# Two token streams of a float32 decoder trunk: products emitted in turn instead of unit by unit, small tiles moved to a pool of their own

## The chip, the cores and the metric

The kernel runs on one core of one Trainium2 chip. The metric is the device time of one execution in microseconds; the median of three runs of the kernel before is 1221.22 us (1220.48 to 1221.98). TensorE (PE in the profile, with its weight loads as PEld) multiplies, VectorE (DVE), ScalarE (ACT) and GpSimd (POOL) do the rest, and SyncE (SP) issues the loads of the weights.

## The reference

Four decoder layers over 256 tokens of width 1024. Layer i has a token mixer of kind i mod 3, then a SwiGLU FFN with 2816 hidden columns; each is wrapped in two RMSNorms:

```python
for i in range(DEPTH):
    kind = i % N_MIXERS
    ...
    hn = rms_norm(x, norm_gains[i, 0])
    if kind == 0:
        m = diff_attention(hn, ...)
    elif kind == 1:
        m = stick_breaking_attention(hn, ...)
    else:
        m = sliding_window_sink_attention(hn, ...)
    x = x + rms_norm(m, norm_gains[i, 1])
    f = swiglu(rms_norm(x, norm_gains[i, 2]), ffn_w_gate[i], ffn_w_up[i], ffn_w_down[i])
    x = x + rms_norm(f, norm_gains[i, 3])
```

Every mixer is an input projection, an attention over 256 keys, and an output projection. All of it is float32, and the weights are read once, some 204 MB.

## The kernel before, in words

**Two streams.** The 256 tokens are two blocks of 128. Stream 0 works on the first block and stream 1 on the second, each through all four layers (`stream`, L900 to L924). Both use the same weights, and the keys and values of the first block are used by the second.

**Products.** A float32 operand is split into two float32r parts, hi and lo, and a product is three matmuls (hi times hi, hi times lo, lo times hi). For the weights, ACT copies a loaded tile into `hi` and DVE writes the rest into `lo` (`split`, L252). For the tokens, `xh` and `xl` (`pre_norm`, L416), `oh` and `ol`, `hTh` and `hTl` (`split_rows`) play the same part. Tokens are the stationary operand, weights the moving one, with 512 columns as a rule.

**Units.** The weights come in units of 128 x 1024 float32, in one list in the order of use (L187 to L236). A unit is loaded by SP into one of 4 stage buffers, split into one of 11 ring buffers, and used by both streams. A unit is 6 matmuls of 512 columns for each stream: in `project` (L494) all 6 add to one PSUM bank (tag `mm`, one bank per stream; the first chunk of a projection uses a bank of the tag `acc`), in `rows_product` (L468) they add to two banks (tag `acc`, two banks per stream), turn by turn. A chunk of a projection is 4 units: 24 matmuls into one bank. An FFN is 11 such chunks, with the down projection of chunk c-1 (2 units) behind chunk c from c = 1 on; the down projections of the last three chunks come at the end.

**The order of the work.** The program is unrolled in Python. Each stream is a generator, and `Emitter.run` (L123) decides which one emits next. A generator yields `("w",)` when it needs its next unit, `("d", ns)` to be resumed no earlier than that many ns of emitted TensorE work later, and `("e", key)` to wait for an event. Between two yields it emits without a break, so that a unit's 6 matmuls come out together. The clock of the emitter, `em.t`, adds 1/2.4 ns per column, 213 ns for a matmul of 512. Attention runs in further generators (tasks) that are resumed as soon as their time or event has come.

Of the two streams, `run` takes the first that can go on, in this order:

```python
behind = any(self.pos[1] < w <= self.pos[0] for w in self.edges)
order = mains[::-1] if behind else mains
```

`pos[s]` is the number of units that stream s has taken. So stream 0 comes first, except while it has passed an edge that stream 1 has not. Edges stand after each layer's input projection (L228) and after each layer's FFN (L236). `can` (L112) lets stream 0 lead by up to LAG = 8 units and lets stream 1 take only units that stream 0 has taken. Around the norms a stream waits: `stream` yields `("d", 4000)` after `post_norm` (L914, L921) and `("d", 600)` after `pre_norm` (L906, L917). There are two norm stops in a layer, one after the mixer and one after the FFN; the last FFN has none behind it, which makes 7.

A scheduler below the emission may still move an instruction past others that it takes to be ready earlier; otherwise each engine runs in the order of emission.

**Where tiles lie.** Tiles are packed in the order of their pools and tags, each padded to a multiple of 32 bytes per partition. Tiles of one to eight floats therefore shift what follows by 32 bytes. In the program of before, the ring's `hi` and `lo`, `oh`, `ol`, `hTh`, `hTl`, and `xh`, `xl` of stream 1 start at multiples of 64 bytes; `xh` and `xl` of stream 0, the identity `ident` (the moving operand of the transposes), its bf16 copy `identb`, the masks and the residual `x` start 32 bytes past one.

**Names in the profile.** `mm_b100q` is the chunk of layer kind b, layer 1, stream 0, group 0, part q. Names that end in digits lose them, so that all FFN chunks of both streams are `mm_f`, all down projections `acc_f`. `th_f` are the FFN's transposes, `tp_n` and `tp_q` those of `pre_norm`, `t_f` and `h_f` the gated activations, `junk_e` the squares in `post_norm` after an FFN, `mg_e` the accumulators times the gain.

Of the kernel before, what the change touches and what calls it, by code (L numbers as in the profile page):

```python
# [9 lines left out]
F32 = mybir.dt.float32  # L10
# [8 lines left out]
P = 128  # L19
# [21 lines left out]
class Emitter:  # L41
    """Orders the emission of several generators by a running estimate of the tensor engine's time.

    A generator yields ("w",) for the next weight unit, ("d", ns) to be resumed no earlier than ns
    after the tensor engine's work emitted so far, or ("e", key) to wait for an event.
    """

    def __init__(self, load_dma, split, n_units, edges):
        self.t = 0.0
        self.load_dma, self.split, self.n, self.edges = load_dma, split, n_units, edges  # L50
        self.issued = self.loaded = 0
        self.pos = [0, 0]
        self.ring = {}
        self.events = set()
        self.limit = 0
        self.tasks = []
# [32 lines left out]
    def run_main(self, m):  # L89
        s = m["s"]  # L90
        value = None
        if m["want"] == "w":
            u = self.pos[s]
            value = self.ring[u]
            self.pos[s] += 1
            if s == 1:
                self.ring.pop(u)
            m["want"] = None
        try:
            what = m["gen"].send(value)  # L100
# [57 lines left out]
def trunk_kernel(ctx, tc, x, positions, norm_gains, a_w_in, a_w_out, a_lambda, a_subln, b_w_in, b_w_out,  # L158
# [5 lines left out]
    wk = ctx.enter_context(tc.tile_pool(name="wk", bufs=2))  # L164
    ps = ctx.enter_context(tc.tile_pool(name="ps", bufs=1, space=PSUM))
# [4 lines left out]
    class Start:  # L170
        """An engine whose instructions stay in the order of emission until the start is over."""
# [40 lines left out]
    def downs(c):  # L212
        """The chunks of the down projection that follow chunk c of the gate and up projections."""
# [55 lines left out]
    pos_i = cst.tile([P, 2], I32, name="pos_i")  # L269
# [10 lines left out]
    nsink = cst.tile([P, 16], F32, name="nsink")  # L280
# [4 lines left out]
    inv = cst.tile([P, 32], F32, name="inv")  # L285
    mhalf = cst.tile([P, 8], F32, name="mhalf")
    quarter = cst.tile([P, 1], F32, name="quarter")
    pool.memset(quarter, math.pi / 2)
    act.activation(wk.tile([P, 1], F32, tag="preload", name="preload", bufs=1), quarter, AF.Sin)
# [7 lines left out]
    # additive masks of a block of keys: causal, strictly causal, and the part of the window before the block  # L297
# [12 lines left out]
    gsub = cst.tile([P, 2], F32, name="gsub")  # L310
    lam_init = [0.8 - 0.6 * math.exp(-0.3 * i) for i in (0, 3)]
    nlam = cst.tile([P, 2], F32, name="nlam")
# [3 lines left out]
    def tables():  # L316
        """Generator: cos twice and sin with its sign, per position."""
        magic = 12582912.0
        posf = cst.tile([P, 2], F32, name="posf")
# [28 lines left out]
    def scalars():  # L348
        """-lambda, the negated sinks, and the gains of the inner norm."""
        lsum = wk.tile([P, 4], F32, tag="lsum", name="lsum", bufs=1)  # L350
# [28 lines left out]
    def mm3(o, ah, al, bh, bl, first, last):  # L379
        mm(o, ah, bh, first, False)  # L380
        mm(o, ah, bl, False, False)
        mm(o, al, bh, False, last)

# [4 lines left out]
    def rstd_of(name, s, ss, more=EPS, extra=None):  # L388
        """1/rms from the mean square, or from two parts of it."""
        u = wk.tile([P, 1], F32, tag=f"u{s}", name=f"u_{name}")  # L390
        r = wk.tile([P, 1], F32, tag=f"r{s}", name=f"r_{name}", bufs=3)
# [4 lines left out]
    def first_halves(s, tps, gs, th, tl, name):  # L396
        """The parts of the first layer's input, between the steps of the tables and the first weights."""
# [57 lines left out]
    def post_norm(s, acc, gain, name):  # L455
        ss = wk.tile([P, 2], F32, tag=f"ssp{s}", name=f"ssp_{name}")
# [23 lines left out]

    def out_proj(s, oT, name, last):
        """Generator: the product of the transposed rows in oT with the next 8 row units, into two banks."""
        acc = None
        for kt in range(KT):
# [6 lines left out]
            rows_product(acc, oh, ol, w, kt == 0, kt == KT - 1)  # L491
# [29 lines left out]
    def scaled_tables(s, r, name):  # L521
        """The tables of the keys, and those of the queries, which carry the scores' scale."""
# [24 lines left out]
    def score_products(s, sc, q, k, mask):  # L547
        """The scores of two pairs of heads: the heads of even and of odd number, in half of the array's rows and a bank each."""
# [13 lines left out]
    def split_rows(oT, sl, src, scale=None):  # L562
        """src, times scale, as two float32r parts."""
# [8 lines left out]
    def layer_a(s, i, xn):  # L572
# [20 lines left out]
        def scores(g):  # L593
# [5 lines left out]
            l = st[g] = wk.tile([P, 2, 4], F32, tag=f"l{s}", name=f"l_{name}{g}", bufs=2)  # L599
            el = st[g, "el"] = wk.tile([P, 4], F32, tag=f"el{s}", name=f"el_{name}{g}", bufs=2)  # L600
            ws = {}
            for step in range(3):
                if step < 2:
# [5 lines left out]
                    nm = wk.tile([P, 2, 2], F32, tag=f"nm{s}", name=f"nm_{name}{g}{h0}")  # L609
# [9 lines left out]
                    r = wk.tile([P, 2], F32, tag=f"rl{s}", name=f"rl_{name}{g}{h0}")  # L619
# [19 lines left out]
        def values(g):  # L639
# [8 lines left out]
            ss = wk.tile([P, 4], F32, tag=f"os{s}", name=f"os_{name}{g}")  # L648
# [124 lines left out]
    def layer_c(s, i, xn):  # L773
# [19 lines left out]
        def heads(chunk, g):  # L793
# [17 lines left out]
            nm = wk.tile([P, 2, 2], F32, tag=f"nm{s}", name=f"nm_{name}{g}")  # L811
            es = wk.tile([P, 2, 2], F32, tag=f"es{s}", name=f"es_{name}{g}")
            l = wk.tile([P, 2, 2], F32, tag=f"l{s}", name=f"l_{name}{g}")
# [43 lines left out]
    def ffn(s, i, xn):  # L857
        name = f"f{i}{s}"
        half = wk.tile([P, 1], F32, tag=f"half{s}", name=f"half_{name}", bufs=1)
        hsq = wk.tile([P, 1], F32, tag=f"hsq{s}", name=f"hsq_{name}", bufs=1)  # L860
# [5 lines left out]
        def down(c):  # L866
            nonlocal acc
            for j in range(2):
# [4 lines left out]
                rows_product(acc, hT[c][0][:, j2, :], hT[c][1][:, j2, :], w, c == 0 and j == 0, c == NCH - 1 and j == 1)  # L873
# [78 lines left out]
```

## Time and profile before

| what | value |
|---|---|
| median of three runs | 1221.22 us |
| the profiled execution, first to last instruction | 1220.4 us |
| what lies around the span, taken as the median less the span | 0.8 us |
| PE busy with matmuls, and their number | 1202.2 us (99%), 6028 |
| DVE, ACT, POOL busy | 64%, 54%, 4% |
| bytes moved | 205.90 MB, 169 GB/s on average |

A row of the groups gives engine, operation, written and read tiles, shape and count, then the busy time in us, the mean ns of one instruction, and the idle time of the engine just before. A matmul's duration covers its whole way through the array, so neighbours overlap; what a matmul costs in a stream is the distance from its start to the next one's start. A row of the chain is start, duration, what ran, and how many; a row of the timeline is start, duration, engine and instruction, with neighbours of one kind merged and, in brackets, the engine's idle time before and what ended it.

### The profile page before, as it was taken

The numbers are of one execution on the slowest core, as the hardware profiler recorded it, in microseconds if no ns is written. First come the engines' busy times: TensorE is split into PE (matmuls) and PEld (weight loads), VectorE is DVE, ScalarE is ACT, GpSimd is POOL, SyncE is SP. The second block draws the span as 40 slices with busy tenths as digits, with TensorE's granted clock in tenths as the row PEclk, the third lists the DMA queues.
The fourth block names the chain that finished last, engine by engine and source line by source line (L and its number), as shares of the span: only waits on it lengthen the run. The fifth ranks groups of instructions, "written<-read, shape, count | busy, mean of one in ns | idle before, by whom it ended". The sixth has DMA issues, their size and how long they took to land.

```text
span 1220.4 us, 16738 instructions
## 1 busy us (share of the span) xinstructions
PE 1202.2 (99%) x6028; PEld 971.7 (80%) x6028; DVE 779.3 (64%) x1217; ACT 656.7 (54%) x1197; POOL 48.1 (4%) x141
## 2 busy tenths in 40 slices
PE   8999999999999999999999999999999999999997
PEld 6787788888878788888888778888878778888886
DVE  7866665555847666555578666555586776655553
ACT  5665644444756654444477664444474565544442
POOL 2000100000200000000000010000010001000000
PEclk9999999999999999999999999999999999999999
DMA  8635465566743546656564246565565453656550
GB/s 274 205 118 157 155 190 184 179 189 183 219 133 121 173 139 189 190 175 187 184 197 137 87 149 187 183 188 182 182 202 151 131 173 121 181 183 189 179 166 35
DMA packets 140838, 205.90 MB, mean 169 GB/s; under 512 B 9554, under 2 KB 104916, under 8 KB 140756
## 3 DMA queue, kind: packets, MB, share of 16 engines
q1 hardware_dynamic: 140048, 204.51, 54.5%
q8 instruction: 47, 0.77, 0.3%
q10 hardware_dynamic: 708, 0.34, 0.1%
q14 instruction: 35, 0.29, 0.1%
HBM read 203.76 MB, written 1.05 MB: 168 GB/s over the span
## 4 chain that ended last, share of the span: by engine, by line
PE 90%; DVE 4%; ACT 2%; issue 1%; DMA 1%; POOL 1%; DVEq 0%; ACTq 0%; POOLq 0%
PE mm_f L180 39%; PE acc_f L180 18%; PE acc_a L180 3%; PE mm_c L180 2%; PE acc_b L180 2%; DVE lo L180 2%; PE sc_a L180 2%; PE th_f L180 2%; PE acc_c L180 1%; PE sc_b L180 1%; ACT hi L180 1%; DMA stage<-in_a_w_in_dram 1%; PE pv_a L180 1%; PE sc_c L180 1%; DVE x L180 1%
## 5 line engine op out<-in xcount | busy, mean ns | idle before, releaser
L180 DVE TENSOR_TENSOR lo<-stage,hi 128x1024 fp32r<-128x1024 f32 x378 | 460.9, 1223 | 297.7 <-ACT hi L180 295.9
L180 ACT ACTIVATE hi<-stage 128x1024 fp32r<-128x1024 f32 x378 | 399.4, 1061 | 333.8 <-PE mm_f L180 160.0
L180 PE MATMUL mm_f<-hi,xh_q 128*128 128x512 f32 x704 | 283.5, 403 | 0.0
L180 PE MATMUL mm_f<-lo,xh_q 128*128 128x512 f32 x704 | 278.6, 396 | 0.0
L180 PE MATMUL mm_f<-hi,xl_q 128*128 128x512 f32 x704 | 221.0, 395 | 0.9 <-DVE xl_q L180 0.9
L180 PEld LDWEIGHTS mm_f<-hi,xl_q 128*128 128x128 f32 x704 | 132.5, 188 | 34.2 <-DVE xl_q L180 1.8
L180 PEld LDWEIGHTS mm_f<-hi,xh_q 128*128 128x128 f32 x704 | 132.3, 188 | 28.7 <-ACT xh_q L180 0.2
L180 PEld LDWEIGHTS mm_f<-lo,xh_q 128*128 128x128 f32 x704 | 132.4, 188 | 28.4
L180 PE MATMUL acc_f<-hi,hTh_f 128*128 128x512 f32 x352 | 114.9, 402 | 0.5 <-ACT hTh_f L180 0.5
L180 PE MATMUL acc_f<-hi,hTl_f 128*128 128x512 f32 x352 | 111.9, 394 | 0.8 <-DVE hTl_f L180 0.8
L180 PE MATMUL acc_f<-lo,hTh_f 128*128 128x512 f32 x352 | 111.5, 392 | 0.0
L180 ACT ACTIVATE t_f<-mm_f,half_f 128x256 f32<-128x256 f32 x88 | 41.8, 475 | 83.6 <-PE mm_f L180 82.6
L180 PEld LDWEIGHTS acc_f<-hi,hTl_f 128*128 128x128 f32 x352 | 65.9, 188 | 16.0 <-DVE hTl_f L180 1.4
L180 PEld LDWEIGHTS acc_f<-lo,hTh_f 128*128 128x128 f32 x352 | 66.1, 188 | 15.3
L180 PEld LDWEIGHTS acc_f<-hi,hTh_f 128*128 128x128 f32 x352 | 63.8, 188 | 13.4 <-ACT hTh_f L180 0.8
L180 DVE SCALAR_TENSOR_TENSOR t_f<-t_f,mm_f 128x256 f32<-128x256 f32 x88 | 36.7, 417 | 37.5 <-ACT t_f L180 37.4
L180 DVE SCALAR_TENSOR_TENSOR h_f<-t_f,hsq_f,mm_f 128x256 f32<-128x256 f32 x88 | 42.2, 480 | 2.7
L180 ACT ACTIVATE hTh_f<-th_f 128x256 fp32r<-128x256 f32 x88 | 33.0, 376 | 18.1 <-PE th_f L180 17.8
L180 DVE TENSOR_TENSOR hTl_f<-th_f,hTh_f 128x256 fp32r<-128x256 f32 x88 | 36.5, 418 | 5.9 <-ACT hTh_f L180 5.9
L180 ACT ACTIVATE e_a<-sc_a,nm_a 128x128 f32<-128x128 f32 (+1 forms) x64 | 26.0, 421 | 17.0 <-DVE nm_a L180 16.9
L180 PEld LDWEIGHTS th_f<-ident,h_f 128*128 128x128 f32 x176 | 24.4, 140 | 11.5
L180 PE MATMUL th_f<-ident,h_f 128*128 128x128 f32 x176 | 33.5, 272 | 0.0
(584 smaller groups left out, 1545.0 us busy)
## 6 DMA issues: line engine op xcount, KB each, us to landing
stage<-in_ffn_w_gate_dram SPq DMA_DIRECT2D x176, 256.0 KB, 2.8
stage<-in_ffn_w_up_dram SPq DMA_DIRECT2D x176, 256.0 KB, 3.1
stage<-in_ffn_w_down_dram SPq DMA_DIRECT2D x88, 512.0 KB, 3.5
stage<-in_a_w_in_dram SPq DMA_DIRECT2D x48, 512.0 KB, 3.9
stage<-in_b_w_in_dram SPq DMA_DIRECT2D x24, 512.0 KB, 3.8
stage<-in_a_w_out_dram SPq DMA_DIRECT2D x16, 512.0 KB, 3.7
stage<-in_c_w_in_dram SPq DMA_DIRECT2D x10, 512.0 KB, 3.8
gain<-in_norm_gains_dram SPq DMA_DIRECT2D x8, 512.0 KB, 4.1
```

The lines of the kernel that those rows point to most:

```text
L180: i = call(*args, **kw)
```

## The change

**The order.** `project` and `rows_product` yield `("m",)` after every matmul. The emitter then notes that it is the other stream's turn, and the order is reversed when the turn is stream 1's. A stream goes on alone only where the other can't. Which bank a matmul adds to is as before, and so are all delays, edges, units and the lead that `can` allows.

**The tiles.** All tiles of under 64 bytes, with `nsink`, `inv` and `mhalf`, move from the pools `cst` and `wk` to a new pool `sm` that lies behind them. The tiles that are left have sizes in multiples of 64 bytes, so that all operands of matmuls start at multiples of 64 bytes. No instruction is added or removed by this.

```diff
@@ class Emitter
+        self.turn = 0
...
         elif what[0] == "e":
             m["want"] = what[1]
+        elif what[0] == "m":
+            self.turn = 1 - s
         else:
             m["want"] = "w"
...
             behind = any(self.pos[1] < w <= self.pos[0] for w in self.edges)
-            order = mains[::-1] if behind else mains
+            order = mains[::-1] if behind or self.turn else mains
...
@@ trunk_kernel
     wk = ctx.enter_context(tc.tile_pool(name="wk", bufs=2))
+    sm = ctx.enter_context(tc.tile_pool(name="sm", bufs=2))
     ps = ctx.enter_context(tc.tile_pool(name="ps", bufs=1, space=PSUM))
...
-    pos_i = cst.tile([P, 2], I32, name="pos_i")
+    pos_i = sm.tile([P, 2], I32, name="pos_i", bufs=1)
...
-        ss = wk.tile([P, 1], F32, tag=f"ss{s}", name=f"ss_{name}")
+        ss = sm.tile([P, 1], F32, tag=f"ss{s}", name=f"ss_{name}")
...
@@ rows_product
         cols = [slice(h * 512, (h + 1) * 512) for h in range(2)]
+        steps = [(h, a, v) for a, v in ((ah, 0), (ah, 1), (al, 0)) for h in range(2)]
         if last:
-            for h, cs in enumerate(cols):
-                mm3(acc[h], ah, al, w[0][:, cs], w[1][:, cs], first, last)
-        else:
-            for v in range(2):
-                for h, cs in enumerate(cols):
-                    mm(acc[h], ah, w[v][:, cs], first and v == 0, False)
-            for h, cs in enumerate(cols):
-                mm(acc[h], al, w[0][:, cs], False, False)
+            steps.sort(key=lambda step: step[0])
+        for h, a, v in steps:
+            mm(acc[h], a, w[v][:, cols[h]], first and v == 0 and a is ah, last and a is al)
+            yield ("m",)
...
@@ project
             for kt, cs in js:
                 for v in range(2):
                     mm(b, xn[0][:, kt, :], w[v][:, cs], kt == 0 and v == 0, False)
+                    yield ("m",)
             for kt, cs in js:
                 mm(b, xn[1][:, kt, :], w[0][:, cs], False, kt == KT - 1)
+                yield ("m",)
```

The two callers of `rows_product`, `out_proj` (L481) and `down` in `ffn` (L866), use `yield from`. The other lines of the diff move further small tiles from `cst` or `wk` to `sm` in the same way.

More of the change, by code (lines that the diff above doesn't have):

```diff
@@ L279, in trunk_kernel @@
     lam_in = wk.tile([P, 2, 2, 2, 64], F32, tag="t2k", name="lam_in", bufs=TMP)
-    nsink = cst.tile([P, 16], F32, name="nsink")
+    nsink = sm.tile([P, 16], F32, name="nsink", bufs=1)
     nc.scalar.dma_start(subr, a_subln)
@@ L283, in trunk_kernel @@
     nc.scalar.dma_start(nsink, c_sinks[0].partition_broadcast(P))
-    inv = cst.tile([P, 32], F32, name="inv")
-    mhalf = cst.tile([P, 8], F32, name="mhalf")
-    quarter = cst.tile([P, 1], F32, name="quarter")
+    inv = sm.tile([P, 32], F32, name="inv", bufs=1)
+    mhalf = sm.tile([P, 8], F32, name="mhalf", bufs=1)
+    quarter = sm.tile([P, 1], F32, name="quarter", bufs=1)
     pool.memset(quarter, math.pi / 2)
-    act.activation(wk.tile([P, 1], F32, tag="preload", name="preload", bufs=1), quarter, AF.Sin)
+    act.activation(sm.tile([P, 1], F32, tag="preload", name="preload", bufs=1), quarter, AF.Sin)
     for j in range(32):
@@ L309, in trunk_kernel @@
     gains = cst.tile([P, P], F32, name="gains")
-    gsub = cst.tile([P, 2], F32, name="gsub")
+    gsub = sm.tile([P, 2], F32, name="gsub", bufs=1)
     lam_init = [0.8 - 0.6 * math.exp(-0.3 * i) for i in (0, 3)]
-    nlam = cst.tile([P, 2], F32, name="nlam")
+    nlam = sm.tile([P, 2], F32, name="nlam", bufs=1)
     cosf = cst.tile([P, 2, 64], F32, name="cosf")
@@ L318, in tables @@
         magic = 12582912.0
-        posf = cst.tile([P, 2], F32, name="posf")
+        posf = sm.tile([P, 2], F32, name="posf", bufs=1)
         r, k, kh, kl, c = (wk.tile([P, 64], F32, tag="t2k", name=f"rt_{n}", bufs=TMP) for n in ("r", "k", "kh", "kl", "c"))
@@ L348, in scalars @@
     def scalars():
-        lsum = wk.tile([P, 4], F32, tag="lsum", name="lsum", bufs=1)
+        lsum = sm.tile([P, 4], F32, tag="lsum", name="lsum", bufs=1)
         lprod = wk.tile([P, 4, 64], F32, tag="t2k", name="lprod", bufs=TMP)
@@ L377, in mm @@
         em.t += n * COLUMN_NS * (4 if f32 else 1)
[L379 to L382, printed above, removed]
     def transpose(o, i):
@@ L388, in rstd_of @@
     def rstd_of(name, s, ss, more=EPS, extra=None):
-        u = wk.tile([P, 1], F32, tag=f"u{s}", name=f"u_{name}")
-        r = wk.tile([P, 1], F32, tag=f"r{s}", name=f"r_{name}", bufs=3)
+        u = sm.tile([P, 1], F32, tag=f"u{s}", name=f"u_{name}")
+        r = sm.tile([P, 1], F32, tag=f"r{s}", name=f"r_{name}", bufs=3)
         pool.tensor_scalar(u, ss, more, extra, ALU.add, *([ALU.add] if extra else []))
@@ L455, in post_norm @@
     def post_norm(s, acc, gain, name):
-        ss = wk.tile([P, 2], F32, tag=f"ssp{s}", name=f"ssp_{name}")
+        ss = sm.tile([P, 2], F32, tag=f"ssp{s}", name=f"ssp_{name}")
         junk = wk.tile([P, D], BF16, tag="junk", name=f"junk_{name}", bufs=1)
@@ L490, in out_proj @@
             oh, ol = (t[:, kt % 4, :] for t in oT[kt // 4])
-            rows_product(acc, oh, ol, w, kt == 0, kt == KT - 1)
+            yield from rows_product(acc, oh, ol, w, kt == 0, kt == KT - 1)
         return acc
@@ L598, in scores @@
             wT[g] = wk.tile([P, 4, nk, P], F32, tag=f"wT{s}", name=f"wT_{name}{g}", bufs=1)
-            l = st[g] = wk.tile([P, 2, 4], F32, tag=f"l{s}", name=f"l_{name}{g}", bufs=2)
-            el = st[g, "el"] = wk.tile([P, 4], F32, tag=f"el{s}", name=f"el_{name}{g}", bufs=2)
+            l = st[g] = sm.tile([P, 2, 4], F32, tag=f"l{s}", name=f"l_{name}{g}", bufs=2)
+            el = st[g, "el"] = sm.tile([P, 4], F32, tag=f"el{s}", name=f"el_{name}{g}", bufs=2)
             ws = {}
@@ L608, in scores @@
                                    lambda kb: masks["causal"] if kb == s else None)
-                    nm = wk.tile([P, 2, 2], F32, tag=f"nm{s}", name=f"nm_{name}{g}{h0}")
+                    nm = sm.tile([P, 2, 2], F32, tag=f"nm{s}", name=f"nm_{name}{g}{h0}")
                     e = [wk.tile([P, 2, nk * P], F32, tag="t2k", name=f"e{c}_{name}{g}{h0}", bufs=TMP) for c in range(2)]
@@ L618, in scores @@
                                                  accum_out=l[:, c, h0 + h:h0 + h + 1])
-                    r = wk.tile([P, 2], F32, tag=f"rl{s}", name=f"rl_{name}{g}{h0}")
+                    r = sm.tile([P, 2], F32, tag=f"rl{s}", name=f"rl_{name}{g}{h0}")
                     dve.reciprocal(r, l[:, 1, hs])
@@ L647, in values @@
                     mm(o[:, h, :], wT[g][:, h, kb, :], V[g, kb][:, h * P:(h + 1) * P], kb == 0, kb == nk - 1, True)
-            ss = wk.tile([P, 4], F32, tag=f"os{s}", name=f"os_{name}{g}")
+            ss = sm.tile([P, 4], F32, tag=f"os{s}", name=f"os_{name}{g}")
             junk = wk.tile([P, D], BF16, tag="junk", name=f"junk_{name}{g}", bufs=1)
@@ L810, in heads @@
             em.set((name, "s", g))
-            nm = wk.tile([P, 2, 2], F32, tag=f"nm{s}", name=f"nm_{name}{g}")
-            es = wk.tile([P, 2, 2], F32, tag=f"es{s}", name=f"es_{name}{g}")
-            l = wk.tile([P, 2, 2], F32, tag=f"l{s}", name=f"l_{name}{g}")
+            nm = sm.tile([P, 2, 2], F32, tag=f"nm{s}", name=f"nm_{name}{g}")
+            es = sm.tile([P, 2, 2], F32, tag=f"es{s}", name=f"es_{name}{g}")
+            l = sm.tile([P, 2, 2], F32, tag=f"l{s}", name=f"l_{name}{g}")
             sink = nsink[:, 4 * g:4 * g + 4].rearrange("p (b j) -> p j b", j=2)
@@ L858, in ffn @@
         name = f"f{i}{s}"
-        half = wk.tile([P, 1], F32, tag=f"half{s}", name=f"half_{name}", bufs=1)
-        hsq = wk.tile([P, 1], F32, tag=f"hsq{s}", name=f"hsq_{name}", bufs=1)
+        half = sm.tile([P, 1], F32, tag=f"half{s}", name=f"half_{name}", bufs=1)
+        hsq = sm.tile([P, 1], F32, tag=f"hsq{s}", name=f"hsq_{name}", bufs=1)
         dve.tensor_scalar(half, xn[2], 0.5, None, ALU.mult)
@@ L872, in down @@
                 j2 = 2 * (c % 2) + j
-                rows_product(acc, hT[c][0][:, j2, :], hT[c][1][:, j2, :], w, c == 0 and j == 0, c == NCH - 1 and j == 1)
+                yield from rows_product(acc, hT[c][0][:, j2, :], hT[c][1][:, j2, :], w, c == 0 and j == 0,
+                                        c == NCH - 1 and j == 1)
             del hT[c]
```

## Prediction

> **What bounds the kernel now.** I read the page first, then who made PE wait, then the chain and the timeline in the stretches that the change touches.
>
> ```profile
> span 1220.4 us, 16738 instructions
> ...
> PE 1202.2 (99%) x6028; PEld 971.7 (80%) x6028; DVE 779.3 (64%) x1217; ACT 656.7 (54%) x1197; POOL 48.1 (4%) x141
> ...
> PEclk9999999999999999999999999999999999999999
> ```
>
> PE is the bound from end to end, at its full granted clock. So only two things can move the time: the distance from one matmul to the next, and time in which PE has nothing to do. The second is small now; of 15 rows of PE's waits these are the ones I use:
>
> ```profile
> PE tp_gain L308 <- DMA rows<-in_norm_gains_dram: 1.8, 1, 1.8
> ...
> PE tp_q L180 <- DVE x L180: 1.2, 4, 0.3
> ...
> PE mm_f L180 <- DVE xl_q L180: 0.9, 2, 0.6
> ...
> PE mm_a000v L180 <- DVE t_a000k L180: 0.6, 1, 0.6
> ```
>
> The start costs 1.8 us, and the norm stops (`tp_q`, `xl_q`) together 2.1 us. This is striking, for a norm stop is a long chain. The timeline at the end of stream 0's first FFN shows it, and the chain shows what hides it:
>
> ```profile
> 313.08 0.39 PE L180 MATMUL acc_f<-hi,hTl_f 128*128 128x512 f32 x1
> ...
> 313.31 0.39 PE L180 MATMUL mm_f<-hi,xh_q 128*128 128x512 f32 x1
> ...
> 314.36 1.28 DVE L180 TENSOR_TENSOR mg_e<-acc_f,gain 128x512 f32<-128x512 f32 x2
> ...
> 315.56 1.41 DVE L180 SCALAR_TENSOR_TENSOR x<-mg_e,r_e,x 128x512 f32<-128x512 f32 x2
> ...
> 321.58 1.04 PE L180 MATMUL tp_n<-ident,x 128*128 128x128 f32 x8
> ...
> 323.32 2.15 ACT L180 ACTIVATE xh_n<-tp_n,gains 128x128 fp32r<-128x128 f32 x8
> ```
>
> ```profile
> 313.48 2.80 PE mm_f L180 x12
> 316.28 5.25 PE acc_f L180 x23
> ...
> 325.39 5.62 PE mm_b100q L180 x24
> ```
>
> Stream 0's last matmul starts at 313.08, its next layer's first (`mm_b100q`) at about 325. In between PE runs 48 matmuls of stream 1, which lags by its full 8 units (x12, x23, and a rest that isn't quoted). Then stream 0 does 24 matmuls alone and hides stream 1's norm. The lead of stream 0 is what keeps PE at 99%.
>
> **Part 1: same bank or another.** The change puts a matmul of the other stream, so of another bank, between two that add to one bank. What that is worth stands in rows where both kinds follow each other:
>
> ```profile
> 1202.30 2.80 PE mm_f L180 x12
> 1205.10 5.01 PE acc_f L180 x22
> ```
>
> ```profile
> 165.92 1.39 PE acc_f L180 x6
> 167.31 1.40 PE mm_f L180 x6
> ```
>
> `mm_f` adds to one bank, `acc_f` to two in turn. The long runs give 2.80 / 12 = 233.3 ns against 5.01 / 22 = 227.7 ns, and `mm_b100q` above 5.62 / 24 = 234.2; the units between the other stream's give 1.40 / 6 = 233.3 against 1.39 / 6 = 231.7. So a neighbour in the same bank costs 1.6 to 6.5 ns. I take 3, nearer to the second pair, since units between the other stream's are what the new order is made of. A unit of a projection has 5 such neighbours; units of 512 columns number 48 (two layers of kind a), 24 (b) and 176 (FFN), for two streams 496, so 2,480 neighbours. I take nine tenths as broken up, 2,230. That is 6.7 us gained, with bounds of 3.6 and 14.5 us.
>
> The Trainium skill ("TensorE: Matmul & The Clock Gate", section "Wait — 56ns, not 53.3ns?") has back-to-back bf16 matmuls of 512 columns at 215.7 ns. The run at 227.7 ns, with two banks and aligned operands, doesn't agree. If the new order came to the page's pace, an estimate from it over some 4,400 matmuls of 512 columns at 233.3 or 231.7 ns would be about 74 us gained, and my sum would end near 1183 us.
>
> **Part 2: the alignment.** Ring, `oh`, `ol`, `hTh`, `hTl` and stream 1's `xh`, `xl` lie at multiples of 64 bytes already. New are stream 0's `xh`, `xl` and `ident`. Stream 0 and stream 1 can be compared in one layer:
>
> ```profile
> 410.64 4.20 PE mm_b111v L180 x18
> ```
>
> Stream 1, aligned: 4.20 / 18 = 233.3 ns; stream 0, 32 bytes off, 234.2 above. At most 0.9 ns over some 1,240 neighbours of stream 0 would be 1.1 us; at the end of the trace stream 1 alone shows the same 233.3. I take 0, with bounds of 0 and 1.1 us gained. Nothing else reads `sm` in another way, and DVE (64%) and ACT (54%) would hide it.
>
> **Part 3: the lead is gone.** This is the part that decides. Today stream 0 is first in the order, so it runs on until it leads by 8 units. With turns, neither gains on the other, and the lead is what the start and the edges leave. At the start stream 1 takes its first unit when stream 0 has done two. The first edge then takes that away: `behind` becomes true when stream 0 has *taken* its last unit before the edge, and since it now pauses after each matmul, stream 1 runs alone until it has taken that unit too. Both then finish the last unit side by side. The same happens at the end of each FFN. Between edges all delays are the same for both. I see no step that builds the lead up again, apart from stream 1's longer attention (two blocks of keys), which may be worth half a unit. So from the first edge on both streams reach each norm stop within a unit of each other (1.40 us), and nothing is left that hides the chain.
>
> The chain in the rows above, alone: from PE's next slot at 313.31 to the first half of `x` (315.56 + 0.7 = 316.3), eight transposes of 1.04 us, with the second half of `x` done at 316.97, and the first eighth of `xh` (2.15 / 8 = 0.27): the first matmul could start at some 317.5. That is 4.2 us, of which about 1 is transposes, so 3.2 us idle. The other stream's norm is on the same engines (another 1.28 + 1.41 on DVE), which delays `xl`: I take 3.5 us. Low bound: a lead of a unit hides 1.4, leaving 1.8; high bound: half of the other's 2.7 on top, 4.6. Seven stops: 24.5 us, bounds 13 and 32. The 2.1 us of today go.
>
> The same holds for smaller waits, four layers each. Chunk 10 of the FFN follows chunk 9 with no down projection between, into the same bank, and the last `down` waits for `hT`:
>
> ```profile
> L180 ACT ACTIVATE t_f<-mm_f,half_f 128x256 f32<-128x256 f32 x88 | 41.8, 475 | 83.6 <-PE mm_f L180 82.6
> ...
> L180 DVE SCALAR_TENSOR_TENSOR h_f<-t_f,hsq_f,mm_f 128x256 f32<-128x256 f32 x88 | 42.2, 480 | 2.7
> L180 ACT ACTIVATE hTh_f<-th_f 128x256 fp32r<-128x256 f32 x88 | 33.0, 376 | 18.1 <-PE th_f L180 17.8
> L180 DVE TENSOR_TENSOR hTl_f<-th_f,hTh_f 128x256 fp32r<-128x256 f32 x88 | 36.5, 418 | 5.9 <-ACT hTh_f L180 5.9
> ```
>
> With a second DVE step like `h_f`, the bank comes free after 0.475 + 2 x 0.48 = 1.4 us, and `hT` takes 0.8: 2.2 us, in four layers 8.8. The scheduler may fill part: 6 us, bounds 0 and 12 (the streams one behind the other). In the mixers of layers 1 to 3, four chunks each start in a bank that their forerunner just filled, and now both streams do so together:
>
> ```profile
> 331.10 0.69 ACT L180 ACTIVATE t_b100q<-mm_b100q,r_n 128x512 f32<-128x512 f32 x1 [0.59 <-PE mm_b100q L180]
> ```
>
> 12 x 0.69 = 8.3 us, and attention's own matmuls fill some: 5 us, bounds 0 and 12.
>
> **Part 4: a cold array behind the gaps.** After the waits of the start, matmuls of 512 columns stand 0.43 us apart, and later 0.23:
>
> ```profile
> 11.91 0.63 PE L180 MATMUL mm_a000q<-hi,xh_n 128*128 128x512 f32 x1
> 12.34 0.63 PE L180 MATMUL mm_a000q<-lo,xh_n 128*128 128x512 f32 x1
> ...
> 15.60 0.39 PE L180 MATMUL mm_a000q<-lo,xh_n 128*128 128x512 f32 x1
> 15.83 0.39 PE L180 MATMUL mm_a000q<-hi,xh_n 128*128 128x512 f32 x1
> ```
>
> From 11.91 to about 15.2 PE works at half the pace, so 1.6 us are lost. If every one of seven gaps led to that, 11 us. The gaps are near the length that might do it and I can't tell from one start: 2 us, bounds 0 and 11. The Trainium skill (same page, "HAM oscillation") says that PE falls back to half clock when it has been idle for a window of some 3.4 us, which speaks against this change. The start agrees in the pace; no run here shows yet what a gap of 3.5 us does in mid-kernel.
>
> **The sum.** -6.7 + 24.5 - 2.1 + 6 + 5 + 2 = +28.7 us on the span of 1220.4, so 1249.1, and with 0.8 around it 1250 us, against the median of 1221.2.
>
> **The rivals.** *The lead survives* (0.16): if something keeps stream 1 at least 2.5 units behind (2.5 x 1.40 = 3.5 us, the idle time of one stop), parts 3 and 4 vanish and the bank gain stays: 1221.2 - 6.7 = 1214.5 us. For it speaks that PE is 99% busy with the same delays; against it the code at the edges. *Every gap goes cold* (0.08): 7 x 1.6 = 11 us for the 2 of part 4, 1259 us; the start speaks for it, and against it that its gaps came when PE had hardly worked yet. This is the rule of the page named in part 4. *The scheduler undoes the turns* (0.06): it moves matmuls by readiness, and if the order came out unit by unit with the old lead, 1221 us; but it has no reason to prefer stream 0.
>
> **How the numbers follow.** My forecast keeps 0.70. Its own range: the low ends, 1221.2 - 14.5 + 13 - 2.1 = 1218, need every bound at once, the high ends 1221.2 - 3.6 + 32 - 2.1 + 12 + 12 + 11 = 1283 as well; I cut both to 1225 and 1275. The range over all cases is 1214 to 1275, which takes in the surviving lead at its forecast. A measurement of this kernel can tell about 0.2% (2.4 us) from no change. Faster: 0.16, less 0.01 for a lead that only half survives, 0.15; same: 0.06; slower: 0.79.
>
> **What would show it.** In the profile after: PE below 99%, with new rows of PE's waits, `tp_q` and `tp_n` <- DVE `x`, 2 to 4 us each and seven times, at which PE's tenths in the 40 slices drop; `mm_f` rows alternating with `mm_f` or `acc_f` of the other stream at 0.230 to 0.231 us; no run of 48 matmuls of stream 1 at an edge; spacings of 0.43 us behind a gap, if part 4 holds. I am wrong if the waits at the norms stay at 2 us (then the lead is there), or if alternating matmuls stand much below 0.228 us or above 0.234 us (then part 1 is mis-sized).

## The result, and the profile after

The changed kernel takes 1255.4 us in the median of four runs (1253.3 to 1257.2), the kernel before 1221.2 (1220.5 to 1222.0): a ratio of 1.0278, with a 95% interval of 1.0263 to 1.0292. The profiled execution is the one of 1253.3 us, with a span of 1251.5 us, 31.1 us longer than that of before.

The page of the changed kernel, in the lines that answer to those of before:

```profile
span 1251.5 us, 16731 instructions
...
PE 1200.9 (96%) x6028; PEld 979.8 (78%) x6028; DVE 770.7 (62%) x1217; ACT 652.7 (52%) x1197; POOL 45.6 (4%) x141
...
PE   8999999999899999999989999999989998999997
...
PEclk9999999999999999999999999999999999999999
```

The same 6028 matmuls keep PE busy for nearly the same time (1200.9 for 1202.2 us), and PE has fallen from 99% to 96%: the new time is idle time, and the four inner slices that have dropped to 8 (at about 313, 626, 907 and 1033 us) hold four of the seven norm stops. What PE waited for (tile, releaser; total, times, longest):

```profile
PE tp_q L185 <- DVE x L185: 10.1, 5, 2.5
PE tp_n L185 <- DVE x L185: 7.6, 4, 2.5
PE acc_f L185 <- ACT hTh_f L185: 3.3, 4, 1.0
...
PE tpr_c L185 <- DVE e_c L185: 1.3, 2, 0.7
PE mm_a301v L185 <- DVE t_a301k L185: 1.2, 1, 1.2
PE mm_a301k L185 <- DVE t_a301q L185: 1.2, 1, 1.2
...
PE ta_b L185 <- DVE b_b L185: 1.0, 2, 0.5
```

The norm stops (`tp_q`, `tp_n`) went from some 2 us to 17.7. Below them stand the end of the FFN (`acc_f` for `hTh_f`), chunks that wait for their bank (`mm_a301k` for DVE's step on the chunk before it), and matmuls of attention that wait for a softmax (`tpr_c`, `ta_b`). The chain of waits shows one stop from end to end, the one after layer 1's mixer (start, duration, what):

```profile
447.39 1.07 ACT hi L185
...
448.48 1.23 DVE lo L185
449.71 0.61 DVE mg_m L185
...
451.06 0.58 POOL r_m L185
...
451.66 0.76 DVE x L185
...
452.56 1.79 PE tp_q L185 x8
454.35 1.71 PE mm_f L185 x4
456.06 0.98 PE tp_q L185 x8
```

No matmul starts between the end of a weight's split (`lo`, at 449.71) and the first transposes: DVE gets to `mg_m` only when `lo` is out of the way, then come POOL and `x`, and PE has nothing else. Behind the stop 8 transposes take 1.79 us and 4 matmuls of 512 columns 1.71 (0.43 each), and then another 8 transposes 0.98: PE comes back at half pace. The windows around the stop before, at 328 us, show the granted clock (the column in front of the last two):

```profile
326.00:328.00 2.00, 0.00 (x0) 0.00 (x0) 1.57 (x4) 2.00 (x6) 0.86 (x2) 1.00 0.64 170
328.00:330.00 2.00, 1.85 (x11) 1.51 (x12) 2.00 (x5) 1.46 (x7) 1.02 (x2) 0.96 0.25 96
330.00:332.00 2.00, 2.00 (x9) 1.46 (x9) 2.00 (x6) 2.00 (x7) 0.00 (x0) 0.50 0.39 162
332.00:334.00 2.00, 2.00 (x9) 1.67 (x8) 2.00 (x9) 2.00 (x10) 0.79 (x2) 0.69 0.26 100
```

The last thing to read is the distance between matmuls of the two streams, in the timeline (start, duration, instruction; `mm_b100q` is stream 0, `mm_b110q` stream 1):

```profile
338.74 0.39 PE L185 MATMUL mm_b100q<-hi,xl_n 128*128 128x512 f32 x1
338.96 0.39 PE L185 MATMUL mm_b110q<-hi,xh_n 128*128 128x512 f32 x1
...
340.78 0.39 PE L185 MATMUL mm_b110q<-hi,xh_n 128*128 128x512 f32 x1
341.00 0.39 PE L185 MATMUL mm_b100q<-lo,xh_n 128*128 128x512 f32 x1
```

Ten distances in 2.26 us are 226 ns, less than any row of before gave me (227.7 in its long runs of `acc_f`). Yet where the new order leaves one stream alone, in one bank, the distance is hardly longer: 229.1 ns in the mean of the 219 neighbours of that kind (distances under 300 ns), against 233.5 before. That doesn't fit the banks. So the experiments had two questions: what made the matmuls faster, and what the turns cost.

### The profile page after: what moved, and what is told of

Same layout as the page of the kernel before. It is cut to its first block, busy times and chain, and to the rows that moved or that the text cites. A ratio compares the mean times of both kernels' runs of the same rounds, so it can differ in the third digit from the quotient of the medians.

```text
span 1251.5 us, 16731 instructions
## 1 busy us (share of the span) xinstructions
PE 1200.9 (96%) x6028; PEld 979.8 (78%) x6028; DVE 770.7 (62%) x1217; ACT 652.7 (52%) x1197; POOL 45.6 (4%) x141
## 4 chain that ended last, share of the span: by engine, by line
PE 66%; issue 23%; DVE 4%; ACT 4%; POOL 1%; DMA 1%; ACTq 0%; DVEq 0%; POOLq 0%
PE mm_f L185 29%; PE acc_f L185 14%; PE acc_a L185 3%; PE acc_b L185 2%; PE sc_a L185 1%; DVE lo L185 1%; PE th_f L185 1%; DMA stage<-in_a_w_in_dram 1%; PE sc_b L185 1%; ACT hi L185 1%; DVE x L185 1%; ACT e_a L185 1%; PE pv_a L185 1%; PE mm_b100q L185 0%; PE mm_a301k L185 0%
## 5 line engine op out<-in xcount | busy, mean ns | idle before, releaser
L185 PE MATMUL mm_f<-hi,xh_q 128*128 128x512 f32 x704 | 235.4, 402 | 0.3 <-ACT xh_q L185 0.2
L185 PE MATMUL mm_f<-lo,xh_q 128*128 128x512 f32 x704 | 222.7, 392 | 0.0
L185 PE MATMUL mm_f<-hi,xl_q 128*128 128x512 f32 x704 | 194.4, 390 | 0.0
L185 PE MATMUL acc_f<-hi,hTh_f 128*128 128x512 f32 x352 | 96.5, 390 | 3.3 <-ACT hTh_f L185 3.3
L185 PE MATMUL acc_f<-hi,hTl_f 128*128 128x512 f32 x352 | 96.2, 390 | 0.0
L185 PE MATMUL acc_f<-lo,hTh_f 128*128 128x512 f32 x352 | 96.0, 389 | 0.0
L185 PEld LDWEIGHTS acc_f<-hi,hTh_f 128*128 128x128 f32 x352 | 65.8, 188 | 17.6 <-ACT hTh_f L185 4.2
L185 ACT ACTIVATE t_f<-mm_f,half_f 128x256 f32<-128x256 f32 x88 | 37.5, 472 | 68.9 <-PE mm_f L185 68.9
L185 DVE TENSOR_TENSOR hTl_f<-th_f,hTh_f 128x256 fp32r<-128x256 f32 x88 | 33.4, 416 | 9.0 <-ACT hTh_f L185 8.5
L185 DVE SCALAR_TENSOR_TENSOR h_f<-t_f,hsq_f,mm_f 128x256 f32<-128x256 f32 x88 | 38.5, 475 | 0.3
L185 ACT ACTIVATE hTh_f<-th_f 128x256 fp32r<-128x256 f32 x88 | 29.2, 374 | 14.1 <-PE th_f L185 13.8
```

Of the source, the lines that this page charges most:

```text
L185: i = call(*args, **kw)
```

## The experiments

My theory for the loss was the missing lead (part 3), for the gain the alternation of banks (part 1). The rivals: the loss comes from the turns themselves; the gain comes from the new addresses.

### The two halves of the change

**Addresses alone.** The tiles of the change, the order of before:

```diff
             what = m["gen"].send(value)
+            while what[0] == "m":
+                what = m["gen"].send(None)
...
-        elif what[0] == "m":
-            self.turn = 1 - s
```

> The tiles as in the change, the emission unit by unit as before, so that only the addresses differ from the kernel before. In the trace of after the matmuls of 512 columns stand 227 ns apart, also where they follow each other in one bank (24 of 258 us in that trace at 226.7 ns), against 233.5 ns in one bank before; worked out from both traces the distances sum to some 29.6 us less. Bank theory (part 1 of the prediction): the neighbours are again in one bank, the distance stays at 233 ns, time 1219 to 1222 us. Address theory: the distance falls to 227 ns with the lead and its cover untouched, time 1221.2 - 29.6 = 1192 us, between 1189 and 1198.

(The bracket in it garbles a count; what it means are runs in one bank, such as 20 distances of `mm_a000k` with a mean of 226.7 ns at 24 us.) Measured: 1205.2 us, ratio 0.9868 (0.9852 to 0.9885). The chain at the place that the prediction quoted, where first stream 1 and then stream 0 (`mm_b100q`) runs alone:

```profile
309.61 2.72 PE mm_f L185 x12
312.33 5.22 PE acc_f L185 x23
...
321.41 5.45 PE mm_b100q L185 x24
```

2.72 / 12 = 226.7, 5.22 / 23 = 227.0 and 5.45 / 24 = 227.1 ns: one bank or two makes no difference any more, and nothing but addresses was changed. The bank theory falls. The gain is 16 us, not 29.6. In the traces of before and of this run, both in the old order, the mean distance of neighbours under 300 ns apart falls from 232.3 to 227.9 ns, which is 17.6 us over some 4,010 of them; my sum had compared two different orders, and what else it counted wasn't worked out.

**Turns alone.** The order of the change, every tile where it lay before:

```diff
-        ss = sm.tile([P, 1], F32, tag=f"ss{s}", name=f"ss_{name}")
+        ss = wk.tile([P, 1], F32, tag=f"ss{s}", name=f"ss_{name}")
...
```

> Turns matmul by matmul as in the change, all tiles where they lay before. Bank theory: the distance falls to 227 to 230 ns by the alternation alone, time 1250 to 1258 us as in the changed kernel. Address theory: the distance stays at 231 to 234 ns and the waits of the lost lead come on top, 1255.4 + 25 to 30 = 1280 to 1285 us. Waits at the norm stops 2.6 us each in both.

Measured: 1265.1 us, 1.0360 (1.0345 to 1.0376). In its timeline the same matmuls as above stand further apart:

```profile
340.71 0.40 PE L184 MATMUL mm_b100q<-hi,xl_n 128*128 128x512 f32 x1
...
343.95 0.39 PE L184 MATMUL mm_b100q<-hi,xl_n 128*128 128x512 f32 x1
```

3.24 us for 14 distances are 231.4 ns. So at the old addresses alternation does bring some 2 ns (233.5 before), but the 226 ns come from the addresses. Between this run and the changed kernel the addresses are worth 9.8 us. The time is 15 to 20 us below what the address theory expected, as that went from 29.6 us too.

### What the turns cost

**The lead given back.** In the changed kernel, stream 0 goes on alone until it leads by 7 units, and finishes a unit at an edge:

```diff
+        m["mid"] = what[0] == "m"
...
-            behind = any(self.pos[1] < w <= self.pos[0] for w in self.edges)
-            order = mains[::-1] if behind or self.turn else mains
+            behind = any(self.pos[1] < w <= self.pos[0] for w in self.edges) and not mains[0]["mid"]
+            order = mains[::-1] if behind or (self.turn and self.pos[0] - self.pos[1] >= 7) else mains
```

> The changed kernel, but stream 0 goes on alone until it leads by 7 units and only then do the streams take turns, and at an edge stream 0 finishes the unit that it has begun before stream 1 goes first. In the order of PE 45 to 48 matmuls of stream 1 then stand behind stream 0's last at each edge, as before the change, where after has 1; seven tenths of the neighbours still alternate. Lead theory (part 3 of the prediction): the rows of PE's waits at the norms fall from 2.5 us each to under 0.6, at the end of the last FFN too, and the time is that of before less what the distance gives: 1192 us, between 1188 and 1200, by either theory of the distance. If the waits come from the alternation itself (both streams' chains on DVE and ACT at once), they stay and the time is 1235 to 1255 us.

Measured: 1228.6 us, 1.0059 (1.0044 to 1.0074). The waits at the norms have fallen, and others have come:

```profile
PE mm_a010v L186 <- DVE t_a010k L186: 2.4, 1, 2.4
...
PE mm_f L186 <- DVE xl_q L186: 2.2, 2, 1.1
PE sc_a L186 <- ACT e_a L186: 2.0, 3, 1.2
PE pv_a L186 <- ACT wT_a L186: 1.9, 2, 1.0
PE tp_q L186 <- DVE x L186: 1.6, 5, 0.4
PE tp_n L186 <- DVE x L186: 1.4, 2, 1.0
PE mm_f L186 <- ACT xh_q L186: 1.4, 2, 0.7
```

The transposes' rows are down from 17.7 to 3.0 us. With the two rows of `mm_f`, whose operands the norm writes, the norms still cost 6.6 us (2.1 before), and the longest wait is 1.1 us where I had expected all under 0.6. Giving back the lead takes away 26.8 of the 50.1 us between the changed kernel and the addresses alone, and 23.4 us stay; the time lies between the two expectations. The same order at the old addresses:

> The same order as the run with a lead of 7 units and turns, all tiles where they lay before. Bank theory: 227 ns where the streams alternate (seven tenths of the neighbours), time 1195 to 1203 us. Address theory: 231 to 234 ns everywhere, time 1217 to 1224 us.

Measured: 1239.1 us, 1.0146 (1.0131 to 1.0161): 10.4 us above its twin, nearly the addresses' worth of the pair before (9.8); both its numbers were set too low by those 23 us, and with them added the time is 1 us under the address theory's range and 13 above the bank theory's.

**Turns in the FFNs only**, with the lead of 7; the mixers' units come out whole:

```diff
...
-    def project(s, xn, n, units_, name, first):
+    def project(s, xn, n, units_, name, first, turns=False):
...
+                    if turns:
+                        yield ("m",)
...
```

> Tiles as in the change; lead of 7 units before the streams take turns, as in the run e3_lead7 (1228.6 us), but turns matmul by matmul only inside the FFNs; the mixers' units come out whole. Mixer theory (the 23 us between e3_lead7 and e1_align_only, 1205.2 us, are lost in the mixers, where both streams' chunk ends and softmax chains fall together; stage lengths of the two traces put the loss there): 1203 to 1207 us. FFN theory (half of the neighbours and more alternate there, so the loss goes with their number): 1215 us or more. If an alternating neighbour has a gain of its own, it shows here with the lead untouched: below 1202 us.

Measured: 1203.7 us, 0.9854 (0.9840 to 0.9869). The mixer theory holds. Alternation with aligned tiles and the lead intact neither costs nor brings anything that the intervals can tell from the addresses alone (0.9868).

**The lead taken away without turns.** The order unit by unit, with `LAG = 1`:

```diff
-LAG = 8
+LAG = 1
```

> Tiles as in the change, emission unit by unit as before, but stream 0 may lead by 1 unit only (LAG 1 for 8), so that 6 matmuls of stream 1 stand behind stream 0's last at an edge, for 48 in e1_align_only (1205.2 us). Lead theory: each of seven norm stops leaves the 2.65 us of after less the 1.36 us of one unit, 1.3 us, in all 9 us, the tail 1 to 2 us more, and the mixers' chunk ends fall nearly together: 1216 to 1235 us. Turns theory (the loss in after comes from alternating matmul by matmul, not from the missing lead): 1205 to 1209 us.

Measured: 1242.5 us, 1.0170 (1.0155 to 1.0185), 37.2 above the addresses alone, more than I had expected of the lead. Counted as in the table below, some 18 us of it lie in the norm stops and some 9 between products of the mixers:

```profile
PE tp_q L185 <- DVE x L185: 7.5, 8, 1.6
PE tp_n L185 <- DVE x L185: 6.7, 5, 2.1
PE mm_a000v L185 <- DVE t_a000k L185: 2.3, 1, 2.3
```

The parts don't add up: the missing lead costs 37.2 us without turns, the turns cost 23.4 with a lead, and both together 50.1. So the 26.8 us above are what the lead is worth where the turns stay, and not its worth by itself.

And with `LAG = 3`:

> As e6_lag1 with a lead of 3 units (18 matmuls, 4.1 us). Lead theory with the threshold that the prediction gave (2.5 units cover a norm stop): the rows at the norms are back to those of e1_align_only, 1205 to 1210 us, the rest being the mixers. If more than the norm chain has to be covered: above 1212 us. Turns theory: 1205 us.

Measured: 1212.9 us, 0.9930 (0.9914 to 0.9947), 7.7 above, in the range that I had set for more than the norm chain. The norms are nearly covered, as 2.5 units of lead were to do (4.1 us in their three rows, 2.4 with the addresses alone); the end of the FFN isn't:

```profile
PE acc_f L185 <- ACT hTh_f L185: 4.1, 4, 1.2
PE tp_q L185 <- DVE x L185: 2.2, 4, 0.6
...
PE mm_f L185 <- ACT xh_q L185: 1.3, 4, 0.3
...
PE tp_n L185 <- DVE x L185: 0.6, 1, 0.6
```

**The edges alone.** The changed kernel with the `mid` rule of above, without the 7 units:

> The changed kernel with the rule at the edges mended alone: stream 1 goes first only when stream 0 isn't within a unit, so that an edge no longer takes stream 0's begun unit away. The prediction blamed this rule for the lost lead, and the lack of any step that builds a lead. If the edges are the cause: the lead of the start survives and the time falls to 1225 to 1240 us. If turns keep any lead at nothing whatever the edges do (in the order of PE 1 to 9 matmuls of stream 1 stand behind stream 0's last at an edge): 1251 to 1257 us, waits at the stops 2.2 to 2.7 us as in after.

Measured: 1250.8 us, 1.0237 (1.0222 to 1.0252). Stop one starts with 0.9 us idle for 2.65, the other six with 2.4 to 2.65 (by the distance of the matmuls around the idle time, less the 0.23 us of one). So the edges aren't what keeps the lead away: with turns nothing builds it.

**The cold array.** The changed kernel with eight transposes in each stop of stream 0:

```diff
+        if s == 0:
+            fill = bank("mm", s, [P, 4, P], f"fill_{name}")
+            for h, q in ((0, 0), (0, 1), (0, 2), (0, 3), (1, 0), (1, 1), (1, 2), (1, 3)):
+                pe.transpose(fill[:, q, :], mg[h][:, q * P:(q + 1) * P], ident)
```

> The changed kernel (1255.4 us) with 8 extra transposes of the scaled accumulators in each norm stop of stream 0, into the bank that is free there: 0.87 us of work for PE inside the idle time of 2.65 us, with an unused result. In the trace of after the granted clock falls to 0.50 behind five of the seven stops, for a loss of 1.7 us each (2 us windows), 8.5 us in all. Cold theory (the drop follows from the length of the idle time): it goes where the idle time is cut in two, and the time falls by 5 to 8.5 us, to 1247 to 1250 us, with the waits at the stops shorter and the same work behind them. If the clock falls for another reason, or if the loss lies in waiting that is there anyway: 1254 to 1257 us.

Measured: 1252.6 us, 1.0249 (1.0234 to 1.0264). The clock stays up, here at the stop at 327 us:

```profile
326.00:328.00 2.00, 1.42 (x10) 1.01 (x11) 1.73 (x3) 1.46 (x6) 0.76 (x3) 1.00 0.68 236
328.00:330.00 2.00, 1.84 (x12) 1.29 (x10) 2.00 (x4) 2.00 (x9) 0.49 (x1) 1.00 0.04 14
330.00:332.00 2.00, 1.79 (x11) 1.15 (x10) 2.00 (x9) 2.00 (x8) 0.79 (x2) 1.00 0.64 248
```

All seven stops show 1.00, so with the idle time filled the drop is gone; but the time fell by 2.7 us only, to between the two expectations. PE isn't busy in the second window and the third (1.84 and 1.79 of 2.00): it now waits for DVE and ACT (2.00), on which stream 1's norm is under way. The changed kernel's own stops agree. From the last matmul of 512 columns ahead of a stop to the 48th behind it take 17.0 to 17.3 us at the five stops with a drop and 16.7 us at the one at 1054 us, where the clock stayed up (the seventh has narrower matmuls behind it); with the eight transposes it is 16.7 us at all six. So the transposes delay nothing, and a drop costs 0.3 to 0.6 us: half pace behind a stop is mostly half pace of work that would have waited.

### Which addresses

**Stream 1's tiles 64 bytes on**, in the order of before:

```diff
+        if s == 1 and n == 0:
+            pool.memset(wk.tile([P, 16], F32, tag="pad", name="pad", bufs=1), 0.0)
```

> As e1_align_only with one unused tile of 64 bytes ahead of stream 1's tiles: stream 0's stationary operands at multiples of 128 bytes, stream 1's at 64 past one, the ring where it was. If a multiple of 64 bytes is what counts, as the change has it: 227 ns for both streams, 1205 us. If it takes a multiple of 128 (before, stream 1's xh and xl lay 64 past one and went at 233.5 ns): 227 ns for stream 0, 232 to 234 for stream 1, 2,328 x 5.6 ns = 13 us on top, 1214 to 1219 us. If the stationary operand has nothing to do with it (the moving one lies 128 past a multiple of 512 bytes in both): 1205 us.

Measured: 1220.6 us, 0.9990 (0.9981 to 0.9999): nearly the whole gain is gone. Stream 1's matmuls and then stream 0's, each alone, in the chain:

```profile
312.70 2.80 PE mm_f L185 x12
315.50 5.37 PE acc_f L185 x23
...
324.77 5.46 PE mm_b100q L185 x24
```

233.3 and 233.5 ns for stream 1, and 227.5 for stream 0's 24 at the end. The tiles were at a multiple of 64 bytes, as the change's words have it, and it didn't help. Stream 0's units between stream 1's pay as well (230.6 ns in the mean), which fits a cost of 15 us in place of the 13 worked out for stream 1's 2,328 alone.

**The weights' ring 64 bytes on**, the tokens' tiles at multiples of 128:

```diff
+    pool.memset(cst.tile([P, 16], F32, name="padc"), 0.0)
+    pool.memset(wk.tile([P, 16], F32, tag="padw", name="padw", bufs=1), 0.0)
```

> As e1_align_only (1205.2 us) with one unused tile of 64 bytes behind the constants and one ahead of the token tiles: the ring of the weights, the moving operands, now starts 64 bytes past multiples of 128, the tokens' tiles, the stationary operands, stay at multiples of 128. If the stationary operand alone counts, as the run with stream 1's tiles 64 bytes off suggests: 227 ns, 1204 to 1207 us. If the moving operand counts as well: 230 ns or more for all units, 1215 to 1235 us.

Measured: 1225.9 us, 1.0036 (1.0023 to 1.0049):

```profile
314.21 2.80 PE mm_f L185 x12
317.01 5.37 PE acc_f L185 x23
...
326.27 5.61 PE mm_b100q L185 x24
```

Now all are slow, stream 0 too (5.61 / 24 = 233.8 ns). **Both 64 bytes on** (the first of the two lines alone):

> As e1_align_only (1205.2 us) with one unused tile of 64 bytes behind the constants: the weights' ring and the tokens' tiles both start 64 bytes past multiples of 128. In every run so far with 233 ns the two operands of a matmul lay differently to a multiple of 128 (0 and 64, 0 and 96, 64 and 0), so that two readings are left. Each operand has to lie at a multiple of 128 bytes: 233 ns or more, 1222 to 1245 us (the run with the ring alone 64 bytes off took 1225.9). The two have only to lie alike: 227 ns, 1204 to 1207 us.

Measured: 1205.0 us, 0.9866 (0.9849 to 0.9882), the best time again, with no operand of these products at a multiple of 128:

```profile
309.26 2.72 PE mm_f L185 x12
311.98 5.22 PE acc_f L185 x23
...
321.05 5.45 PE mm_b100q L185 x24
```

So what counts is how the two operands of a matmul lie to each other. Alike: 227 ns. 64 or 96 bytes apart to a multiple of 128: 233 ns.

## Why the prediction was right or wrong

The time was inside the range and 5.4 us above the forecast, but that it came so near is luck: the gain of part 1 was 10 us too small, and 12 us of loss, in attention and at the end, had no term. To set this out I added up, for each matmul in the traces, the distance to the next one less the lower quartile of such distances for its operation (226 to 227 ns for 512 columns), each put where it ends; a stop counts from 1 us ahead of the first transpose of the stream that comes first to 9 us behind it.

| us in the trace | before | addresses alone | after | lead of 7 and turns |
|---|---|---|---|---|
| first 25 us | 6.6 | 6.7 | 6.5 | 5.8 |
| the seven norm stops | 5.5 | 4.8 | 30.8 | 10.8 |
| the FFNs, without their ends | 31.3 | 17.8 | 17.2 | 18.8 |
| last `down` of an FFN behind `th_f` | 0.8 | 0.8 | 4.2 | 0.8 |
| mixers, product to product | 11.5 | 9.2 | 16.2 | 11.7 |
| mixers, the rest (attention) | 63.0 | 62.7 | 72.6 | 77.7 |
| sum | 118.7 | 102.0 | 147.5 | 125.6 |
| behind the last matmul's start | 6.6 | 6.6 | 8.9 | 6.6 |
| span | 1220.4 | 1203.7 | 1251.5 | 1227.3 |

The sums with the last matmul's row differ by as much as the spans: -16.7 from before to the addresses alone, +47.8 from there to after.

**Part 1 and part 2 (-6.7 and 0): wrong in the cause, and too small by 10 us (-16.7 in the order of before).** The step that failed is the comparison in part 1: "`mm_f` adds to one bank, `acc_f` to two in turn". They differ in a second thing: `acc_f` has `hTh` and `hTl` as stationary operand, which lay like the ring to a multiple of 128, `mm_f` has `xh` and `xl`, which lay 96 (stream 0) and 64 (stream 1) past one. The run with the addresses alone is 227 ns in one bank. Part 2 then compared stream 0 with stream 1, found 234.2 and 233.3 ns, and read this as "alignment brings nothing", when both were among the slow ones; equal rows on both sides of a suspected threshold show nothing if the threshold lies elsewhere. The second pair of part 1 (233.3 against 231.7 ns) fits this too: the `acc_f` units in it stood among `mm_f` units, as stream 0's units did among stream 1's in the run with 230.6 ns. My own sign for the error was in the text, alternating matmuls much below 0.228 us: they came out at 0.226.

The Trainium skill ("TensorE: Matmul & The Clock Gate", section "Wait — 56ns, not 53.3ns?") has 215.7 ns for 512 columns of bf16. The float32r products of these runs came no nearer to it than 226 to 227 ns, so the rival sum of 1183 us had no ground here.

**Part 3, the norm stops (+24.5 - 2.1), with part 4 (+2): right.** The three come to 24.4 us; the table has 30.8 - 4.8 = 26.0. The mechanism was right, and that the sums agree so well is partly luck. Each stop's first idle time was 2.55 to 2.65 us (by distance, as above) in place of the 3.5 I took, 18 us in all. The other 12 to 13 us of the 30.8 lie behind it, where the clock is down and stream 1's norm holds DVE and ACT, and there I had put 2. That the lead is the cause is shown from both sides: given back, it takes the stops to 10.8, taken away without any turn (`LAG = 1`) it brings waits of 14.2 us there, and with 3 units 4.1 us are left. The blame on the edges was wrong: mending them changed one stop of seven.

**Part 4 alone (2, bounds 0 and 11): right.** The clock fell behind five of seven stops, and keeping it up brought 2.7 us. The other three executions of the changed kernel, at a mean clock of 0.985 to 0.986 for 0.992 in the profiled one, lost some 8 us more of clock by that mean and are 2 to 4 us longer; where they lost it no trace shows. So the median stands above the profiled run. The Trainium skill (same page, section "HAM oscillation — how this bites in real kernels") lets PE fall to half clock in idle times above some 3.4 us; here 2.4 to 2.5 us between two matmuls in the rows (2.55 to 2.65 by distance) were enough at five stops of seven, so the measurement decides against that length.

**Part 3, the small waits (+6 and +5): about right in sum.** The ends of the FFNs cost 3.4 us; the bank of chunk 10, which I had added there, shows nothing. The mixers' products cost 7.0, with the rows of `mm_a301k` and its like among them.

**Not in the prediction: attention (+9.9) and the tail (+2.3).** At the very end both streams' last norms follow each other, where before stream 0's was long done: 8.9 us behind the last matmul's start for 6.6. And attention's own matmuls wait for softmax steps. This is the part that the lead doesn't cure: with 7 units of lead and turns it is even 15 us above the addresses alone, with `LAG = 1` and no turns only 2.8 us (65.5 for 62.7). At that lead it comes from turns in the mixers, for without those it is gone (60.9 in the run with turns in the FFNs only); for the changed kernel itself that is argued, not shown. Why exactly the softmax chains come out later in that order, whether by the delays counted in emitted work or by both streams' chains on ACT and DVE at once, wasn't separated and stays open.

**The rivals.** The lead did not survive; the turns were not undone; the drops of the clock were there, but cheap. What none of them held is a kernel below both: the addresses without the turns, 1205 us.

## What to carry to other kernels

An alternation on the instruction level takes away the lead that one stream has over the other, and with it what hides each serial chain; look first for who covers the chain, then for the nanoseconds. Before a difference between two groups of matmuls is put down to one property, list all in which they differ, the addresses among them: here the two tile families differed in banks and in addresses at once. And split a change of two parts on the chip, for here one half was worth -16 us and the other +50 at the new addresses.

## What the runs showed of the hardware

- Float32r matmuls of 512 columns with a stationary operand of 128 x 128 stood 227 ns apart when both operands lay alike to a multiple of 128 bytes (both at 0, or both at 64), and 233 ns when they lay 64 or 96 bytes apart. `hTh` of stream 0 lay 256 bytes off the ring to a multiple of 512 in the run with turns alone, and `acc_f` had its 227 to 228 ns there; an offset of 128 was in no run, so that a period of 256 isn't excluded.
- A unit that lay well, between units that didn't, was slowed as well: 230.6 ns in the mean for stream 0 in the run with stream 1's tiles 64 bytes on, and 227.5 in its run of 24 matmuls.
- The number of banks made no difference at the good addresses: 227.9 ns for neighbours in one bank, 227.8 for others, over the 4,011 neighbours under 300 ns apart of the run with the addresses alone.
- Each of the five drops of the granted clock behind a stop summed to 1.7 us of lost clock over the windows of 2 us, as in 3.4 us at half, and cost 0.3 to 0.6 us of time. Eight transposes in the idle time kept it from falling at all seven stops.
- At the start the granted clock reads 1.00 (12 to 14 us in the trace of before), although matmuls of 512 columns stand 0.43 us apart there, as they do at a reading of 0.50 behind a stop. So the column doesn't show what slows that first stretch.
